# A softmax with relative bias: chunks of 6 rows in 4 buffers instead of 4 in 6, an evenly shared first load, and a drain of GpSimd's queue ahead of the end

## Chip, cores, metric

One core of a Trainium2 chip, all other cores idle. The metric is the device time of one execution in microseconds (us). "Span" is the time from the first to the last instruction in the profile; the measured time is some 1.6 to 2.0 us longer.

## The reference

```python
B, H, S = (2, 8, 2112)          # logits [B, H, S, S] float32, rel_bias [H, 33]
rel = clip(pos[:, None] - pos[None, :], -16, 16) + 16
x = logits + rel_bias[:, rel][None]
out = softmax(x, axis=-1)       # float32
```

Input and output are 285.5 MB each, so every element is loaded once and stored once: 571 MB in all.

## The kernel before

16 matrices of 2112 rows lie on 128 partitions, 264 rows to a partition. A chunk is `R` rows of every partition, in one of `BUFS` buffers. GpSimd's queue issues the loads, SyncE's the stores; VectorE adds the bias and scales, ScalarE takes exponentials with row sums. Within a chunk the work goes in parts of two rows, so that VectorE adds one part while ScalarE works on another. The maximum is not subtracted.

```python
    R = 4
    PARTS = [(0, 2), (2, R)]
    BUFS = 6
    N = T // R                       # T = 264 rows per partition
    ...
    def vec(eng, u, start, loads):   # VectorE
        eng.wait_ge(loaded[u], loads)
        for r0, r1 in PARTS:
            add(eng, u, r0, r1, start)
        for r0, r1 in PARTS:
            take(eng, summed, 1)
            ... reciprocal of the row sums ...
            for i in range(r0, r1):
                e = eng.tensor_scalar_mul(...)
        e.then_inc(scaled, 1)
    ...
    def sync_part(eng):
        row_load(eng, 0, R // 2, first)        # rows 0, 2 of the first chunk
        row_load(eng, 1, R // 2 - 1, first)    # row 1
        eng.wait_ge(loaded[BUFS - 2], 16)
        passes(eng, 0, lambda u, start, loads: store(eng, u, start))
        for n in range(BUFS):
            take(eng, stored[n], 16)

    def gpsimd_part(eng):
        row_load(eng, R - 1, 1, loaded[0])     # row 3
        ... two iotas ...
        for n in range(1, BUFS):
            if n == BUFS - 1:
                take(eng, made, 1)             # the last buffer is scratch until the bias strip is made
            load(eng, n, n * R)
        passes(eng, BUFS, lambda u, start, loads: reload(eng, u, start))
```

`take` waits for a semaphore and takes the count away again; `reload` waits until a buffer is stored and loads it anew. ScalarE's queue loads the small bias table first, VectorE makes the bias strip `F` out of it, and only then can the first add start.

Of the kernel before, what the change touches and what calls it, by code (L numbers as in the profile page):

```python
# [14 lines left out]
def kernel(  # L15
# [20 lines left out]
    P = 128  # L36
    B, H, S, S2 = logits.shape
# [4 lines left out]
    T = S // Q  # L42
    assert Q * B * H == P and T * Q == S and T % W == 0
    M = T // W
    R = 4
    PARTS = [(0, 2), (2, R)]
    BUFS = 6
    N = T // R
    assert N * R == T and N % BUFS == 0 and R % 2 == 0
    FW = S + T - 1  # L50
    NB = (FW - 2 * MR) // W
    assert NB * W + 2 * MR == FW
    RS = R * S

# [3 lines left out]
    one = const.tile([P, 1], FP32, tag="one", name="one")  # L58
    L = [const.tile([P, RS], FP32, tag=f"L{u}", name=f"L{u}") for u in range(BUFS)]
    tot = [const.tile([P, R], FP32, tag=f"tot{u}", name=f"tot{u}") for u in range(BUFS)]  # L60


    qi, mm, qm, eq, lt, gt, rest = (
        L[BUFS - 1][:, NB * m : NB * (m + 1)] for m in range(7)
    )
# [8 lines left out]
    section = ctx.enter_context(tc.tile_critical(name="rows"))  # L74
    loaded = [nc.alloc_semaphore(f"loaded{u}") for u in range(BUFS)]
    stored = [nc.alloc_semaphore(f"stored{u}") for u in range(BUFS)]
    table = nc.alloc_semaphore("table")
    blocks_ready = nc.alloc_semaphore("blocks_ready")
    strip = nc.alloc_semaphore("strip")
    first = nc.alloc_semaphore("first")  # L80
# [6 lines left out]
    def take(eng, sem, v):  # L87
        eng.wait_ge(sem, v).then_inc(sem, -v)  # L88

    def load(eng, u, start):  # L90
        eng.dma_start(out=L[u][:], in_=rows(logits, start)).then_inc(loaded[u], 16)  # L91

    def store(eng, u, start):
        take(eng, scaled, 1)
        eng.dma_start(out=rows(out, start), in_=L[u][:]).then_inc(stored[u], 16)

    def reload(eng, u, start):
        take(eng, stored[u], 16)
        load(eng, u, start)

    def add(eng, u, r0, r1, start):
        x = L[u]
        x3 = bass.AP(
            tensor=x.tensor,
            offset=x.offset + (r1 - 1) * S,
            ap=[[list(x.ap[0])[0], P], [-S, r1 - r0], [1, S]],
        )

        F3 = bass.AP(
            tensor=F.tensor,  # L110
            offset=(F.offset + T - r1) - start,
            ap=[[list(F.ap[0])[0], P], [1, r1 - r0], [1, S]],
        )
        eng.tensor_tensor(out=x3, in0=x3, in1=F3, op=ALU.add).then_inc(added, 1)  # L114

    def exps(eng, u):
        for r0, r1 in PARTS:
            take(eng, added, 1)
            for i in range(r0, r1):
                x = L[u][:, i * S : (i + 1) * S]  # L120
                e = eng.activation(out=x, in_=x, func=EXP, accum_out=tot[u][:, i : i + 1])  # L121
            e.then_inc(summed, 1)

    def vec(eng, u, start, loads):
# [5 lines that stand above are left out]
            t = tot[u][:, r0:r1]  # L130
            eng.reciprocal(out=t, in_=t).then_inc(inverted, 1)  # L131
            take(eng, inverted, 1)
            for i in range(r0, r1):
                x = L[u][:, i * S : (i + 1) * S]
                e = eng.tensor_scalar_mul(out=x, in0=x, scalar1=tot[u][:, i : i + 1])  # L135
        e.then_inc(scaled, 1)

    def passes(eng, n0, body):

        with eng.Fori(0, ((N - n0) // BUFS - 1) * 8 + 1, 8) as i:  # L140
            for n in range(n0, n0 + BUFS):
                body(n % BUFS, i * (BUFS * R // 8) + n * R, i * 2 + 16 * (n // BUFS + 1))

# [3 lines left out]
    def strip_of(eng):  # L147

        assert M * Q & (M * Q - 1) == 0
        low = rbP[:, W - 1 : W]  # L150
        high = rbP[:, 0:1]
        pitch = list(F.ap[0])[0]
        blocks = bass.AP(tensor=F.tensor, offset=F.offset + MR, ap=[[pitch, P], [W, NB], [1, W]])
        rev = bass.AP(
            tensor=rbP.tensor,
            offset=rbP.offset + W - 1,
            ap=[[list(rbP.ap[0])[0], P], [0, NB], [-1, W]],
        )

        def wide(t):  # L160
            return bass.AP(
                tensor=t.tensor, offset=t.offset, ap=[[list(t.ap[0])[0], P], [1, NB], [0, W]]
            )

        def step(ins):
            ins.then_inc(strip, 1)
            take(eng, strip, 1)

        take(eng, blocks_ready, 2)
        step(eng.tensor_single_scalar(out=qi, in_=qi, scalar=M * Q - 1, op=ALU.bitwise_and))  # L170
        step(eng.tensor_tensor(out=qm, in0=qi, in1=mm, op=ALU.subtract))  # L171
        for m, op in ((eq, ALU.is_equal), (lt, ALU.is_gt), (gt, ALU.is_lt)):
            step(eng.tensor_scalar(out=m, in0=qm, scalar1=0.0, scalar2=None, op0=op))  # L173
        take(eng, table, 16 * B)
        step(eng.tensor_scalar(out=rest, in0=lt, scalar1=low, scalar2=None, op0=ALU.mult))  # L175
        step(eng.tensor_copy(out=F[:, 0:MR], in_=low.to_broadcast([P, MR])))  # L176
        step(
            eng.scalar_tensor_tensor(  # L178
                out=rest, in0=gt, scalar=high, in1=rest, op0=ALU.mult, op1=ALU.add
            )  # L180
        )
        step(eng.tensor_copy(out=F[:, FW - MR : FW], in_=high.to_broadcast([P, MR])))  # L182
        step(eng.tensor_tensor(out=blocks, in0=wide(eq), in1=rev, op=ALU.mult))  # L183
        step(eng.tensor_tensor(out=blocks, in0=blocks, in1=wide(rest), op=ALU.add))  # L184
        eng.sem_inc(made, 1)

    def table_load(eng, bs):
        for b in bs:
            eng.dma_start(
                out=rbP[b * H * Q : (b + 1) * H * Q],  # L190
                in_=bass.AP(
                    tensor=rel_bias.tensor,
                    offset=rel_bias.offset,
                    ap=[[W, H], [0, Q], [1, W]],
                ),
            ).then_inc(table, 16)

    def row_load(eng, r0, m, sem):

        x = L[0]  # L200
        eng.dma_start(  # L201
            out=bass.AP(
                tensor=x.tensor,
                offset=x.offset + r0 * S,
                ap=[[list(x.ap[0])[0], P], [2 * S, m], [1, S]],
            ),
            in_=bass.AP(
                tensor=logits.tensor,
                offset=logits.offset + r0 * S,
                ap=[[T * S, P], [2 * S, m], [1, S]],  # L210
            ),
        ).then_inc(sem, 16)

    def sync_part(eng):

        row_load(eng, 0, R // 2, first)
        row_load(eng, 1, R // 2 - 1, first)
        eng.wait_ge(loaded[BUFS - 2], 16)
        passes(eng, 0, lambda u, start, loads: store(eng, u, start))
        for n in range(BUFS):  # L220
            take(eng, stored[n], 16)

    def gpsimd_part(eng):
        row_load(eng, R - 1, 1, loaded[0])
        eng.iota(qi, pattern=[[0, NB]], base=0, channel_multiplier=M).then_inc(  # L225
            blocks_ready, 1
        )
        eng.iota(mm, pattern=[[1, NB]], base=1 - M, channel_multiplier=0).then_inc(  # L228
            blocks_ready, 1
        )  # L230
        for n in range(1, BUFS):
            if n == BUFS - 1:
                take(eng, made, 1)
            load(eng, n, n * R)
        passes(eng, BUFS, lambda u, start, loads: reload(eng, u, start))

    def scalar_part(eng):
        table_load(eng, range(B))


        eng.activation(  # L241
            out=one, in_=nc.const_aps.tensor(0.0, [P, 1], FP32), func=EXP
        )
        passes(eng, 0, lambda u, start, loads: exps(eng, u))

    def vector_part(eng):
        strip_of(eng)
        take(eng, first, 32)
        passes(eng, 0, lambda u, start, loads: vec(eng, u, start, loads))

    sync_part(nc.sync)
    gpsimd_part(nc.gpsimd)
    scalar_part(nc.scalar)
    vector_part(nc.vector)


# [28 lines left out]
```

## Time and profile before

| | before |
|---|---|
| time, median of the first 3 runs | 1335.5 us (1335.49 to 1335.8) |
| span of the profiled run | 1333.3 us |
| VectorE / ScalarE busy | 72% / 40% |
| DMA, 200 to 1200 us | 433 GB/s, busy share 1.00 |
| last store landed / span ends | 1326.9 / 1333.3 us |

The page's DMA issues (queue and shape, KB each, median us from issue to landing):

```profile
out_dram<-L SPq DMA_DIRECT2D x66, 4224.0 KB, 71.0
L<-in_logits_dram POOLq DMA_DIRECT2D x65, 4224.0 KB, 31.8
```

A store takes 71 us from issue to landing. Shared with the loads its own transfer takes 20 us (10 alone), so some 2.5 stores are queued ahead of it. The windows view of the last stretch (us; busy time of VectorE, ScalarE, GpSimd; clock; DMA share; GB/s) shows what that queue is good for:

```profile
1290.00:1300.00 10.00, 7.76 (x7) 6.09 (x8) 0.00 (x0) 1.00 1.00 433
1300.00:1310.00 10.00, 0.00 (x0) 0.00 (x0) 0.00 (x0) 1.00 1.00 433
```

While VectorE finishes the last chunk (1290 to 1300) and for 20 us after it, DMA goes on at full rate out of the queue.

### The profile page before, as it was taken

The numbers are of one execution on the slowest core, as the hardware profiler recorded it, in microseconds if no ns is written. First come the engines' busy times: TensorE is split into PE (matmuls) and PEld (weight loads), VectorE is DVE, ScalarE is ACT, GpSimd is POOL, SyncE is SP. The second block draws the span as 40 slices with busy tenths as digits, with TensorE's granted clock in tenths as the row PEclk, the third lists the DMA queues.
The fourth block names the chain that finished last, engine by engine and source line by source line (L and its number), as shares of the span: only waits on it lengthen the run. The fifth ranks groups of instructions, "written<-read, shape, count | busy, mean of one in ns | idle before, by whom it ended". The sixth has DMA issues, their size and how long they took to land. A line of the windows view has us; busy time of VectorE, ScalarE, GpSimd; clock; DMA share; GB/s. (4 is left out here: it accounts for less than half of the span.)

```text
span 1333.3 us, 2515 instructions
## 1 busy us (share of the span) xinstructions
DVE 954.7 (72%) x539; ACT 529.8 (40%) x530; POOL 37.0 (3%) x72
## 2 busy tenths in 40 slices
DVE  2888888777677677677677677677677677677670
ACT  0444455444244244244244244344344343343340
POOL 1000000000000000000000000000000000000000
DMA  9999999999999999999999999999999999999996
GB/s 396 430 432 425 437 436 425 437 436 436 426 436 438 424 437 436 435 427 436 438 423 438 437 434 427 436 438 424 437 437 433 428 437 437 424 438 436 434 427 286
DMA packets 19571, 570.99 MB, mean 428 GB/s; under 512 B 2289, under 2 KB 2289, under 8 KB 2289
## 3 DMA queue, kind: packets, MB, share of 16 engines
q1 hardware_dynamic: 9920, 288.72, 50.2%
q0 software_dynamic: 9504, 282.24, 49.1%
q10 hardware_dynamic: 144, 0.02, 0.0%
q14 instruction: 3, 0.02, 0.0%
HBM read 285.49 MB, written 285.47 MB: 428 GB/s over the span
## 5 line engine op out<-in xcount | busy, mean ns | idle before, releaser
L121 ACT ACTIVATE L<-L 128x2112 f32<-128x2112 f32 x264 | 516.0, 1955 | 763.8 <-ACTq L88 763.8
L114 DVE TENSOR_TENSOR L<-L,F 128x4224 f32<-128x4224 f32 x132 | 595.7, 4554 | 201.0 <-DMA L<-in_logits_dram 200.2
L135 DVE TENSOR_SCALAR L<-L,tot 128x2112 f32<-128x2112 f32 x264 | 337.0, 1318 | 21.4 <-DVEq L88 6.1
L131 DVE RECIPROCAL tot<-tot 128x2 f32<-128x2 f32 x132 | 21.3, 162 | 98.3 <-DVEq L88 98.3
L91 POOL DMA_DIRECT2D L<-in_logits_dram x65 | 35.9, 552 | 1213.3 <-POOLq L88 1213.3
L121 ACT ACTIVATION_READ_ACCUMULATOR L<-L 128x1 f32 x264 | 49.2, 186 | 0.0
L175 DVE TENSOR_SCALAR L<-L,rbP 128x71 f32<-128x71 f32 x1 | 0.3, 258 | 19.9 <-DVEq L88 19.9
L183 DVE TENSOR_TENSOR F<-L,rbP 128x2343 f32<-128x2343 f32 x1 | 2.6, 2599 | 0.1
L184 DVE TENSOR_TENSOR F<-F,L 128x2343 f32<-128x2343 f32 x1 | 2.6, 2599 | 0.1
L241 ACT ACT_TABLE_LOAD x1 | 1.3, 1283 | 2.9 <-issue 2.9
L170 DVE TENSOR_SCALAR L<-L 128x71 int32<-128x71 int32 x1 | 0.2, 198 | 2.9 <-DVEq L88 2.9
L173 DVE TENSOR_SCALAR L<-L 128x71 f32<-128x71 f32 x3 | 0.7, 239 | 0.4
L201 POOL DMA_DIRECT2D L<-in_logits_dram x1 | 0.7, 664 | 1.1 <-PEq L280 1.1
L178 DVE SCALAR_TENSOR_TENSOR L<-L,rbP 128x71 f32<-128x71 f32 x1 | 0.3, 294 | 0.2 <-DVEq L88 0.2
L171 DVE TENSOR_TENSOR L<-L 128x71 f32<-128x71 int32 x1 | 0.2, 235 | 0.1
L182 DVE COPY F<-rbP 128x16 f32<-128x16 f32 x1 | 0.2, 175 | 0.1
L176 DVE COPY F<-rbP 128x16 f32<-128x16 f32 x1 | 0.2, 174 | 0.1
L225 POOL IOTA L<- 128x71 int32 x1 | 0.2, 208 | 0.1
L228 POOL IOTA L<- 128x71 int32 x1 | 0.2, 208 | 0.0
L241 ACT ACTIVATE one<-const-float32-0.0 128x1 f32<-128x1 f32 x1 | 0.2, 203 | 0.0
L269 POOL MEMSET const-float32-0.0<- 128x1 f32 x1 | 0.1, 99 | 0.4 <-issue 0.4
L269 POOL MEMSET const-bfloat16-1.0<- 128x1 bf16 x1 | 0.1, 102 | 0.0
(2 smaller groups left out, 0.2 us busy)
## 6 DMA issues: line engine op xcount, KB each, us to landing
out_dram<-L SPq DMA_DIRECT2D x66, 4224.0 KB, 71.0
L<-in_logits_dram POOLq DMA_DIRECT2D x65, 4224.0 KB, 31.8
L<-in_logits_dram SPq DMA_DIRECT2D x1, 2112.0 KB, 10.2
L<-in_logits_dram SPq DMA_DIRECT2D x1, 1056.0 KB, 22.6
L<-in_logits_dram POOLq DMA_DIRECT2D x1, 1056.0 KB, 10.1
rbP<-in_rel_bias_dram ACTq DMA_DIRECT2D x2, 8.2 KB
```

Source lines behind the costliest of these rows:

```text
L91: eng.dma_start(out=L[u][:], in_=rows(logits, start)).then_inc(loaded[u], 16)
L114: eng.tensor_tensor(out=x3, in0=x3, in1=F3, op=ALU.add).then_inc(added, 1)
L121: e = eng.activation(out=x, in_=x, func=EXP, accum_out=tot[u][:, i : i + 1])
L131: eng.reciprocal(out=t, in_=t).then_inc(inverted, 1)
L135: e = eng.tensor_scalar_mul(out=x, in0=x, scalar1=tot[u][:, i : i + 1])
L173: step(eng.tensor_scalar(out=m, in0=qm, scalar1=0.0, scalar2=None, op0=op))
L175: step(eng.tensor_scalar(out=rest, in0=lt, scalar1=low, scalar2=None, op0=ALU.mult))
L178: eng.scalar_tensor_tensor(out=rest, in0=gt, scalar=high, in1=rest, op0=ALU.mult, op1=ALU.add)
L183: step(eng.tensor_tensor(out=blocks, in0=wide(eq), in1=rev, op=ALU.mult))
L184: step(eng.tensor_tensor(out=blocks, in0=blocks, in1=wide(rest), op=ALU.add))
L201: eng.dma_start(out=bass.AP(tensor=x.tensor, offset=x.offset + r0 * S, ap=[[list(x.ap[0])[0], P], [2 * S, m], [1, S]],), in_=bass.AP(tenso ...
L241: eng.activation(out=one, in_=nc.const_aps.tensor(0.0, [P, 1], FP32), func=EXP)
```

## The change

The intent: fewer and larger transfers with the same SBUF (24 rows of buffer either way), a first chunk that both queues bring in equal halves, and GpSimd's queue drained as soon as its last load is issued.

```diff
-    R = 4
-    PARTS = [(0, 2), (2, R)]
-    BUFS = 6
+    R = 6
+    PARTS = [(0, 2), (2, 4), (4, R)]
+    BUFS = 4
@@ row_load: m rows, two apart -> R // 2 rows, two apart
@@ sync_part
-        row_load(eng, 0, R // 2, first)
-        row_load(eng, 1, R // 2 - 1, first)
+        row_load(eng, 0, first)
@@ gpsimd_part
-        row_load(eng, R - 1, 1, loaded[0])
+        row_load(eng, 1, loaded[0])
         ...
         passes(eng, BUFS, lambda u, start, loads: reload(eng, u, start))
+        eng.drain()
@@ vector_part
-        take(eng, first, 32)
+        take(eng, first, 16)
```

More of the change, by code (lines that the diff above doesn't have):

```diff
@@ L196, in table_load, with row_load @@
             ).then_inc(table, 16)
-    def row_load(eng, r0, m, sem):
+    def row_load(eng, r0, sem):
         x = L[0]
@@ L204, in row_load @@
                 offset=x.offset + r0 * S,
-                ap=[[list(x.ap[0])[0], P], [2 * S, m], [1, S]],
+                ap=[[list(x.ap[0])[0], P], [2 * S, R // 2], [1, S]],
             ),
@@ L209, in row_load @@
                 offset=logits.offset + r0 * S,
-                ap=[[T * S, P], [2 * S, m], [1, S]],
+                ap=[[T * S, P], [2 * S, R // 2], [1, S]],
             ),
```

## The prediction

> **What bounds the kernel now.** I read the page first, for which engine is full:
>
> ```profile
> span 1333.3 us, 2515 instructions
> DVE 954.7 (72%) x539; ACT 529.8 (40%) x530; POOL 37.0 (3%) x72
> ...
> DMA  9999999999999999999999999999999999999996
> ```
>
> VectorE is at 72%, ScalarE at 40%, and the DMA engines are busy in every slice but the last. The windows view puts figures on a middle stretch and on the end:
>
> ```profile
> 600.00:620.00 20.00, 14.36 (x8) 8.00 (x8) 0.53 (x1) 1.00 1.00 433
> ...
> 1313.00:1318.00 5.00, 0.00 (x0) 0.00 (x0) 0.00 (x0) 1.00 1.00 433
> 1318.00:1323.00 5.00, 0.00 (x0) 0.00 (x0) 0.00 (x0) 1.00 0.64 277
> 1323.00:1328.00 5.00, 0.00 (x0) 0.00 (x0) 0.00 (x0) 1.00 0.03 14
> 1328.00:1333.00 5.00, 0.00 (x0) 0.00 (x0) 0.00 (x0) 1.00 0.00 0
> ```
>
> The last columns are the DMA share and GB/s. The share is 1.00 at 433 GB/s with loads and stores mixed (600) and with stores alone (1313). 571 MB at 433 GB/s is 1,318.7 us, nearly the span. The rest is a start of about 2.2 us (the first packet in the trace's records starts at 2.2) and an end in which nothing moves: DMA falls off at about 1321.5, yet the span lasts to 1333.3. Twelve microseconds at the end want an explanation. Line 74 (the close of the critical section), asked for by itself, gives half of it:
>
> ```profile
> L74 ACTq DRAIN  x1: 13/13/13, 1327.0 to 1327.0; - x1
> L74 POOLq DRAIN  x1: 5446/5446/5446, 1327.0 to 1327.0; - x1
> L74 DVEq DRAIN  x1: 17/17/17, 1327.0 to 1327.0; - x1
> ```
>
> (min/median/max in ns, then first and last start.) All engines drain at 1327.0, and only GpSimd's takes 5.446 us. The DMA queue's waits agree:
>
> ```profile
> SPq L74 <- POOLq L74: 5.3, 1, 5.3
> ```
>
> So the end reads: 15 of 16 DMA engines finish the last store by 1323.2 and the sixteenth at 1326.9 (the increments of that store's semaphore), then 5.4 us of GpSimd drain, then 0.8 us of closing barriers. The measured 1335.5 is 2.2 us above the span; I take that as constant.
>
> VectorE is no bound: it waits for loads, short and often, in the waits view:
>
> ```profile
> DVE L L114 <- DMA L<-in_logits_dram: 200.2, 52, 3.9
> ```
>
> The kernel is therefore bound by the transfers themselves. A saving counts only at the head, in the tail, or per packet.
>
> **What the Trainium skill says.** (1) "DMA: Bandwidth & Descriptors", section "Where 436 GB/s comes from", gives a ceiling of 435.2 GB/s for 16 ports, and "Why small descriptors are slow (HBM only)" a fixed overhead of about 3 cycles per packet. The trace agrees in kind. By its packet records a packet of 8,448 B takes 319 ns and one of 33,792 B takes 1,251 ns (medians). The difference, 932 ns for 25,344 B, is 27.2 GB/s for one engine, 435 GB/s for 16, and leaves 8.4 ns fixed per packet: more than three cycles, but small. So size barely matters, and it is already known what a bigger packet can give. (2) Same page, section "Queues, rings and completion order": each DMA engine takes turns between queues, a packet at a time. The head agrees: the tiny table waits behind large packets and lands at 24.4 us. (3) "Perfetto Trace Analysis", section "Sequencer-only Instruction (DRAIN, etc)": the reported time of a DRAIN starts when its semaphore wait is satisfied. So 5.446 us is execution, not waiting. I found no page that says why GpSimd's drain is long after DMA issues. (4) "DMA: Bandwidth & Descriptors", section "Latency and other measured facts", says that engines 7 and 15 are usually slower. The trace has one engine that lags (3.7 us on the last store); it does not show which.
>
> **The change part by part.**
>
> *Drain ahead of the end.* GpSimd has nothing left after its last load (issued at 1251.26). A drain placed there runs beside some 70 us of transfers. The one at line 74 remains, but has nothing new to do; GpSimd's further drains in the closing barriers take 34 to 78 ns. Gain: 5.4 us, all on the path that sets the end.
>
> *Bigger chunks: packets.* A chunk has 8 partitions per DMA engine (128/16) and each partition's run is one packet. Before: 33,792 B; after: 6 x 8,448 = 50,688 B, by the two durations above 319 + 5 x 310.7 = 1,872 ns, my estimate. Per engine before: first chunk 4 x 8 = 32 packets of 319 ns = 10.2 us; then 65 loads and 66 stores x 8 = 1,048 x 1.251 = 1,311.0; sum 1,321.3. After: 48 x 0.319 = 15.3; (43 + 44) x 8 = 696 x 1.872 = 1,303.2; sum 1,318.5. Gain 2.8 us. The 4-byte semaphore packets (9 ns) fall from 134 to about 89 per engine: 0.4 us. Together 3.2 us, on the path, because DMA is the bound.
>
> *Bigger chunks: VectorE and ScalarE.* The same 132 adds of 4.55 us, 264 multiplies of 1.32 us and 264 exponentials of 1.96 us. Where chunks are not starved, VectorE has fewer chunk ends at which it waits for ScalarE (1.5 us each at present). All of this lies beside transfers: nothing.
>
> *First chunk shared evenly.* Now three rows on each queue, all in small packets. The table's 18 small packets per participating engine wait one round each; a round is 0.32 + 0.32 us while both queues hold small packets, instead of 0.32 + 1.25 us later on. I expect the table at about 16 us instead of 24.4, the first add at about 24 instead of 32.2, and the first store ready near 24 + 22 = 46. SyncE then waits for chunk 2 (18 rows, 19.5 MB at 433 GB/s: 45 us, so about 48). The fourth load, issued at 24, keeps DMA busy meanwhile: it was busy before and is busy after. Gain on the path: nothing. The extra small packets are in the sum already.
>
> *Four buffers: does DMA ever run out?* A period is 24 rows, 120 us, as before. A chunk is 22.8 us in the engines (worked out below), so about 97 us of each buffer's period are in DMA, and one chunk takes 30 us in each direction when both are mixed: about three chunks are always queued. No.
>
> *Tail.* Here it is tight. Before, the last chunk was:
>
> ```profile
> 1283.40 9.03 DVE L114 TENSOR_TENSOR L<-L,F 128x4224 f32<-128x4224 f32 x2 [3.88 <-DMA L<-in_logits_dram]
> ...
> 1297.01 2.55 DVE L135 TENSOR_SCALAR L<-L,tot 128x2112 f32<-128x2112 f32 x2
> 1299.80 0.33 SPq L95 DMA_DIRECT2D out_dram<-L  x1
> ```
>
> Landing (1283.1) to store was 16.7 us; the stores then queued lasted far longer. After: three adds end at 13.6; the third exponential pair runs 13.7 to 17.7; multiplies of parts one and two fill 13.9 to 19.4; the third reciprocal and multiplies end at 22.3; with the two hand-overs (0.28, 0.24) 22.8 us, plus about 1.1 to the first packet: 24. Work left when the last load lands: a store completes about 10 to 12 us ahead of each load landing (11 to 12.5 in the trace), so the next store has had half of that in DMA time, leaving 15 - 5.5, plus one whole store of 15: about 24.5 us. Just covered. I allow +0.3 us, with 2 us possible.
>
> Sum: 1335.5 - 5.4 - 3.2 + 0.3 = 1327.2.
>
> **Rivals.** *The early drain buys nothing*: the long drain may be a cost of waking GpSimd after a long idle, or of anything that follows its DMAs, so that the last drain is long again. The only long drain in the trace is both first after DMA issues and after 75 us of idleness, so the trace cannot tell. The short ones that follow directly speak for "nothing new to do". I give this rival one in five; it makes the time 1332.6.
>
> *The tail opens*: with only four buffers, the load's latency may come out longer, and fewer stores are left to hide 24 us of compute. DMA would stand idle for 1 to 3 us late. One in four: 1328 to 1330.
>
> *Packets of 50,688 B are slower, or are cut*: nothing in the trace has this size. Cut in two they would give 25,344 B packets of 0.94 us, 1.33 times as many as before instead of two thirds: 1,392 x 0.940 = 1,309 us instead of 1,303, some 6 us worse than predicted. If the row pitch in HBM met some conflict it could be 2% or more; but 33,792 B packets show none. One in twelve.
>
> *The faster start pays on the path*: for it, 8 us of earlier compute; against it, the DMA share of 1.03 and 1.05 in the windows from 10 to 30 us, when compute does not run at all. Worth 0.
>
> *The lagging engine*: it sets the end, 3.7 us behind the fifteenth. Its lag grows in the mixed stage only; if per packet, it shrinks by a third (-1 us), if per turn between large packets it grows by half (+2).
>
> **Range and chances.** The main case is 1327.2, with about 1 us either side for lag and packets; the drain rival and the open tail stretch the upper side to 1332.5. I give 1327.3, 1324.8 to 1332.6. Two per cent is 26.7 us: faster would need 1308.8, and 571 MB at 435.2 GB/s alone take 1,312, so it is out of reach; slower needs a fault of the large packets. Faster 0.01, within 0.97, slower 0.02.
>
> **What would show it.** A short GpSimd drain at line 74 (under 0.1 us) and a long one at the new line, 70 us or more ahead of the end: the drain step right. 33,792 B records replaced by 50,688 B ones of 1.87 us, and some 435 GB/s in the middle: the packet step. First add near 24 us with an unchanged DMA share in the first 50 us: the head is worth nothing. DMA share 1.00 from the last load's landing until the fall, and the last store issued before the previous one lands: no hole in the tail. I am wrong if the time is above 1333 (drain and packets both void), or below 1324 (something saved that I do not see).

## The result, and the profile after

| | before | after |
|---|---|---|
| time, median (range) | 1335.49 us (1333.25 to 1335.8, 4 runs) | 1328.0 us (1325.86 to 1330.2, 4 runs) |
| ratio, 95% interval | | 0.9948 (0.9925 to 0.997) |
| span of the profiled run | 1333.3 | 1328.6 |
| time of the profiled run | 1335.23 | 1330.2 |

A ratio is the mean time of one kernel's fast runs over that of the other's of the same rounds, so it is not quite the ratio of the medians quoted beside it. Two later calls (chips 7 and 11) ran the same changed kernel again: medians 1329.89 and 1330.02, beside 1335.51 and 1335.76 for the kernel before, so the gain there is 5.6 to 5.7 us and not 7.5. The 15 runs of the changed kernel spread from 1325.9 to 1335.4, those of the kernel before from 1332.9 to 1336.6. The profile below is of the slowest of the first four runs, which is near the later medians; no run near 1326 was traced.

The page of the changed kernel:

```profile
span 1328.6 us, 2321 instructions
...
DVE 946.9 (71%) x539; ACT 529.8 (40%) x530; POOL 44.0 (3%) x50
...
DMA  9999999999999999999999999999999999999997
...
out_dram<-L SPq DMA_DIRECT2D x44, 6336.0 KB, 53.7
L<-in_logits_dram POOLq DMA_DIRECT2D x43, 6336.0 KB, 42.7
```

Still DMA-bound, with the same work on VectorE. A store now takes 53.7 us, of which its own transfer is 30 when shared (15 alone): only 0.8 of a store is queued ahead of it, 12 us of work instead of 25. Line 74, where the critical section closes, and line 238, the added drain (ns, then start in us):

```profile
L74 POOLq DRAIN  x1: 47/47/47, 1327.5 to 1327.5; - x1
```

```profile
L238 POOLq DRAIN  x1: 45987/45987/45987, 1244.6 to 1244.6; - x1
```

The long drain has moved: it runs from 1244.6 to 1290.6, beside the transfers, and the one at the end takes 0.047 us. The same middle stretch (200 to 1200 us) asked of the DMA view, first of the kernel before, then of the changed one:

```profile
DMA packets 14421, 433.05 MB, mean 433 GB/s; under 512 B 1606, under 2 KB 1606, under 8 KB 1606
```

```profile
DMA packets 9628, 433.69 MB, mean 434 GB/s; under 512 B 1072, under 2 KB 1072, under 8 KB 1072
```

A third fewer packets move 0.15% more bytes in the same 1000 us. Over 1,320 us that would be 2.0 us, not the 3.2 predicted; but the window is a coarse measure, as c_r4_rest (below), with the packets of the kernel before, moved 433.39 MB in it, half of the difference. The head came earlier as foretold: by the timeline the first add starts at 25.05 us instead of 32.23. And the tail, in the windows view:

```profile
1290.00:1300.00 10.00, 10.00 (x3) 5.85 (x5) 0.00 (x0) 1.00 1.01 436
1300.00:1310.00 10.00, 9.55 (x10) 6.15 (x8) 0.00 (x0) 1.00 0.46 198
1310.00:1315.00 5.00, 0.81 (x1) 0.00 (x0) 0.00 (x0) 1.00 0.76 324
```

From 1300 to 1310, where the kernel before ran at 433 GB/s with its compute already done, the changed one moves less than half of that while VectorE is still at the last chunk. This is a hole. The timeline gives its cause: the last chunk's first add waits for its load until 1289.0, and its last multiplies end at 1310.8.

```profile
1289.00 13.50 DVE L114 TENSOR_TENSOR L<-L,F 128x4224 f32<-128x4224 f32 x3 [8.17 <-DMA L<-in_logits_dram]
...
1308.26 2.55 DVE L135 TENSOR_SCALAR L<-L,tot 128x2112 f32<-128x2112 f32 x2
```

The increments of the store semaphores tell how the 16 DMA engines stand (each store raises its semaphore in 16 steps, which I read as one for each engine whose share has landed):

| | first | 15th | 16th |
|---|---|---|---|
| before, last store but one | 1311.75 | 1313.25 | 1316.94 |
| before, last store | 1321.72 | 1323.21 | 1326.90 |
| after, last store but one | 1305.04 | 1307.31 | 1311.29 |
| after, last store | 1327.22 | 1327.37 | 1327.40 |

After the change, all engines wait for the last store, which is issued at 1311.04; its first packets start at 1311.9. The fastest engine has been idle for about 7 us by then, the slowest for 1.1 (both from the packet records). So the hole costs the end only what the slowest engine sees of it.

**Where the 4.7 us of span went.** A store of 6 rows takes 15.0 us alone. Without hole, the fastest engine would have ended at 1305.0 + 15.0 = 1320.0 instead of 1321.7: 1.7 us less transfer time, which every engine has. The slowest would have ended at 1311.3 + 15.0 = 1326.3 instead of 1326.9: its lag behind the fastest has grown from 5.2 to 6.2 us, which takes back 1.1. The hole takes the other 1.1: the store lands at 1327.4. So transfers and tail together end 0.5 us **later** than before. All that is gained in the span comes after them: from landing to the end of the span 6.4 us before, 1.2 after, which is the drain's 5.4 less 0.2 of closing steps that it had covered. 0.3 us more is gained outside the span (time minus span 1.95 before, 1.65 after). The drain is not the reason, as a_drain_only and c_r4_rest (4 rows, with the drain) have 2.05; what is, no run shows.

### The profile page after: what moved, and what is told of

The parts are those of the page before. It is cut to its first block, busy times and chain, and to the rows that moved or that the text cites. A ratio compares the mean times of both kernels' runs of the same rounds, so it can differ in the third digit from the quotient of the medians.

```text
span 1328.6 us, 2321 instructions
## 1 busy us (share of the span) xinstructions
DVE 946.9 (71%) x539; ACT 529.8 (40%) x530; POOL 44.0 (3%) x50
## 5 line engine op out<-in xcount | busy, mean ns | idle before, releaser
L91 POOL DMA_DIRECT2D L<-in_logits_dram x43 | 42.6, 991 | 1200.0 <-POOLq L88 1200.0
L204 POOL DMA_DIRECT2D L<-in_logits_dram x1 | 0.9, 880 | 1.1 <-PEq L283 1.1
## 6 DMA issues: line engine op xcount, KB each, us to landing
out_dram<-L SPq DMA_DIRECT2D x44, 6336.0 KB, 53.7
L<-in_logits_dram POOLq DMA_DIRECT2D x43, 6336.0 KB, 42.7
```

Source lines behind the costliest of these rows:

```text
L91: eng.dma_start(out=L[u][:], in_=rows(logits, start)).then_inc(loaded[u], 16)
L204: eng.dma_start(out=bass.AP(tensor=x.tensor, offset=x.offset + r0 * S, ap=[[list(x.ap[0])[0], P], [2 * S, R // 2], [1, S]],), in_=bass.AP( ...
```

## The experiments

All twelve runs were timed in 5 rounds beside the kernel before, in three calls (a_, b_, c_, each on another chip), and every result was correct. Theory at the start: the drain is worth its 5.4 us, the packets about 2, and the hole in the tail costs about 1 and makes the times scatter. Rivals: the drain's gain comes from elsewhere (fewer transfers, or the head); the packets are worth the predicted 3.2; the scatter has nothing to do with the hole.

### a_change: the changed kernel again

> The whole change again, on this chip, to see how much the times spread from run to run on one chip. If the two levels seen so far (1326 and 1330) belong to the chip, these runs agree within 1 us; if they belong to the run, both levels show here. The trace should again have a DMA hole of about 1 us on the slowest DMA engine and 5 to 7 us on the others before the last store.

Measured: 1329.89 us (1328.77 to 1332.89, 5 runs; before 1335.51; ratio 0.996, 0.9948 to 0.9973). A scatter of 4 us is there on one chip, so that much belongs to the run; but the level of 1326 did not come back in these runs or in the six of c_change, so of the two levels this settles nothing. In this trace the slowest engine had no hole (it finished the last store but one at 1312.1, after the last store's issue at 1309.95); the fastest idled from 1304.9 on. Lag first to last 6.85 us. So in these two traces the time is about the same with and without a hole on the slowest engine (spans 1328.6 and 1328.2): where there was no hole, the lag was larger.

### a_drain_only

```diff
 (kernel before)
         passes(eng, BUFS, lambda u, start, loads: reload(eng, u, start))
+        eng.drain()
```

> The kernel before with nothing but the drain added. Theory (drain leaves the end): 5.4 us faster than before, about 1330.1, with a GpSimd drain under 0.1 us at the close of the critical section. Rival (the long drain belongs to any drain that follows a long idle): same time as before, and a drain of about 5.4 us still there.

Measured: 1330.54 us (1330.4 to 1331.14; ratio 0.9963, 0.995 to 0.9976), 5.0 us less than before. Its lines 74 and 236 (the drain):

```profile
L74 POOLq DRAIN  x1: 47/47/47, 1327.5 to 1327.5; - x1
```

```profile
L236 POOLq DRAIN  x1: 34518/34518/34518, 1251.8 to 1251.8; - x1
```

The theory holds, the rival of a wake-up after idleness falls: GpSimd has been idle for 41 us ahead of its last drain here, and it is short. One added line gives nearly the whole difference between the two kernels.

### a_no_drain

```diff
 (changed kernel)
-        eng.drain()
```

> The change without the drain. Theory: 5.4 us slower than the change, about 2 us faster than before. If the length of the drain goes with the number of GpSimd's transfers since the start (45 instead of 66), the last drain takes about 3.7 us; if it is a constant, 5.4 us.

Measured: 1334.51 us (1330.48 to 1341.25, 6 runs; ratio 1.0001, 0.9981 to 1.0022): 4.6 us slower than the change by the medians, and no different from the kernel before. The 2 us below the kernel before that I had expected did not show; with runs that lie 11 us apart they are not ruled out either. The drain at the end:

```profile
L74 POOLq DRAIN  x1: 3652/3652/3652, 1327.0 to 1327.0; - x1
```

At these two counts the length goes with the number of transfers that GpSimd issued: 3,652 ns for 44, 5,446 ns for 66, both 83 ns each (the count is 1 row load and 43 loads here, 1 and 65 before). So larger chunks alone would have shortened the end by 1.8 us, and the early drain takes the remaining 3.65. Where the drain is placed behind the last load, it ends 1.85 us (44 transfers, changed kernel) or 2.74 us (66, a_drain_only) after that load has landed, so 42 ns for each: it waits for the transfers that are under way. A third count shows that this is no general rule: in c_r2_rest (below), with 132 transfers, the drain ended 1.28 us after the last load had landed, and not 5.5.

### a_even_only

```diff
 (kernel before)
-        row_load(eng, 0, R // 2, first)
-        row_load(eng, 1, R // 2 - 1, first)
+        row_load(eng, 0, R // 2, first)
@@
-        row_load(eng, R - 1, 1, loaded[0])
+        row_load(eng, 1, R // 2, loaded[0])
@@
-        take(eng, first, 32)
+        take(eng, first, 16)
```

> The kernel before with nothing but the even split of the first chunk (2 rows and 2 rows). Theory (DMA is the bound from the first microseconds): table and first add come several us earlier, the time stays within 1 us of before. Rival (an earlier start of VectorE reaches the end): 5 us or more faster.

Measured: 1336.19 us (1335.57 to 1337.04; ratio 1.0005, 0.9992 to 1.0017). The timeline shows that the head did what it should, 9 us ahead of the kernel before:

```profile
23.21 9.03 DVE L114 TENSOR_TENSOR L<-L,F 128x4224 f32<-128x4224 f32 x2 [0.81 <-DVEq L88]
```

And nothing of it reached the end (0.7 us slower by the medians, within the interval). The even split is worth nothing, as predicted.

### b_split_store

The last pass is written out behind the loop (SyncE and VectorE), and the last chunk is stored by parts:

```diff
 (changed kernel, last chunk)
-        store(eng, u, start)
+        for r0, r1 in PARTS:
+            take(eng, scaled, 1)         # given after each part's multiplies
+            eng.dma_start(out=rows(out, (N - 1) * R + r0, (r1 - r0) * S),
+                          in_=L[BUFS - 1][:, r0 * S : r1 * S]).then_inc(stored[BUFS - 1], 16)
```

> The change, with the last chunk's store cut into three, each sent as soon as its two rows are scaled, so the last 15 us of stores start some 6 us sooner after the last load lands. Theory (a hole ahead of the last store, 0 to 1.4 us on the slowest DMA engine and 5 to 7 us on the others, is what makes the change's runs scatter): no hole in the trace on any engine longer than 1 us, 0 to 1.5 us faster than the change (1328.5 to 1330), and runs that agree within 1.5 us instead of 4. Rival (the scatter comes from elsewhere): the same scatter of 4 us, no gain.

Measured: 1329.36 us (1328.81 to 1333.41; ratio 0.9959, 0.9946 to 0.9972). The hole is smaller, 313 GB/s in place of 198; on the fastest engine it is 2.9 us instead of 7, still more than the 1 us that I had allowed:

```profile
1300.00:1310.00 10.00, 9.55 (x9) 7.75 (x8) 0.00 (x0) 1.00 0.73 313
1310.00:1315.00 5.00, 2.40 (x2) 0.00 (x0) 0.00 (x0) 1.00 1.00 426
```

The scatter stayed at 4.6 us, so my theory of the scatter falls. The profiled run was the slowest of the five (1333.41), and in it two engines came late: the last store but one had its first increment at 1305.3, its 15th at 1314.5 and its 16th at 1315.7. The lag of one or two engines differs from trace to trace, and in this run it set the time: 15.0 us of stores after 1315.7 end at 1330.6, where the last increment came. That it moves the time of the untraced runs too is likely, not shown. By the medians the closed hole gains 0.5 to 0.7 us over the change of the other two calls, which is within the scatter.

### b_act_loads and b_act_split

All loads move from GpSimd's queue to ScalarE's; the reload for chunk n + 2 is issued after the exponentials of chunk n. The second kernel has the split store as well.

```diff
 (changed kernel, scalar_part, abridged)
-        passes(eng, 0, lambda u, start, loads: exps(eng, u))
+        for n in range(2):
+            exps(eng, n)
+        passes(eng, 2, both)             # both: exps(u); reload((u + 2) % BUFS, start + 2 * R)
+        for n in range(N - 2, N):
+            exps(eng, n % BUFS)
```

> The change with all loads issued from ScalarE's queue (hardware descriptors) instead of GpSimd's; GpSimd issues no transfer and is not drained. Theory (one DMA engine lags 4 to 6 us behind because of GpSimd's descriptors): all 16 increments of the last stores and loads come within about 1 us, and the time falls by the lag, 3 to 5 us below the change, to 1325 to 1327. Rival (the lag belongs to the DMA engine or to where the data lies): the last increment still comes 3 to 5 us after the fifteenth, and the time is that of the change, about 1330.

> Both: loads from ScalarE's queue and the last store in three pieces. Without the lag the hole ahead of the last store would stand open on all engines (some 1 to 3 us), so the split should give that on top of b_act_loads: 1323 to 1325. If the lag stays, about as b_split_store.

Measured: b_act_loads 1332.84 us (1329.22 to 1335.95, 6 runs; ratio 0.9979), b_act_split 1329.72 us (1329.25 to 1331.48; ratio 0.9961). The lag did not go; in this the rival was right, while the time of b_act_loads was nearer 1333 than its 1330. In the profiled run of b_act_loads the last store but one had its 15th increment at 1306.3 and its 16th at 1314.8, a lag of 8.5 us with no GpSimd transfer in the kernel; in b_act_split 4.2 us. In this trace the lag is also what makes the hole:

```profile
1300.00:1310.00 10.00, 9.85 (x5) 9.07 (x11) 0.00 (x0) 1.00 0.42 182
1310.00:1315.00 5.00, 4.70 (x7) 2.03 (x3) 0.00 (x0) 1.00 0.05 20
```

The last load has landed only when the slowest engine has brought its share (1294.1 here, ten us after the fastest), so compute starts late, and all engines but one run dry. So here the lag is paid a second time, as little is queued behind the last load.

### b_row_packets

Every store is cut into two strided halves (even rows, odd rows), so its packets are single rows of 8,448 B.

> The change with every store in two strided halves, so that stores move in packets of 8,448 B and not 50,688 B: 1,760 more packets per DMA engine, nothing else changed. With 8.4 ns per packet (the records' durations, as predicted) 14.8 us slower than the change; with 5.2 ns (durations less the 3 ns by which neighbouring records overlap) 9.2 us; with nothing per packet, the same time.

Measured: 1346.32 us (1345.34 to 1349.34; ratio 1.0086, 1.0073 to 1.0099), 16.4 us slower than a_change of another call, more than either figure. The middle stretch:

```profile
DMA packets 31079, 427.61 MB, mean 428 GB/s; under 512 B 1583, under 2 KB 1583, under 8 KB 1583
```

The packet records split the 16.4. Load packets (50,688 B, unchanged) take longer than 1,872 ns by 158 us in sum over 16 engines, 9.9 us per engine; in the changed kernel 1.1. The longer ones, by 0.1 to 0.7 us for the most part, are nearly all (454 of 472) the last packet of a load on its engine. A load of large packets now lands in a median of 23.7 us beside stores of small ones (42.7 in the changed kernel), and then the load queue is empty until the next load. Why the last packets take longer is not shown. If they lengthen the run by their mean, they account for 8.8 us. The remaining 7.6 over 1,760 packets (44 more semaphore packets per engine are in it) are 4.3 ns per packet. This fits how the records lie: within one DMA engine the next packet's record starts most often 4 ns before the last one ends, so of the 8.4 ns that the durations give, 4.4 are left. The experiment is less clean than it was meant to be, as it changed the sharing of the queues too; so the 4.3 ns is an estimate from the records, not a measurement by itself.

### c_change, c_r4_rest

The change once more, and the change with `R`, `PARTS` and `BUFS` as before.

> The change once more, as the partner of the other runs of this call: about 1330, with a scatter of some 4 us.

> The change with the chunk size alone put back to 4 rows in 6 buffers (drain and even split stay). Theory (the fewer packets save 1.8 us on every DMA engine, but the slowest engine's larger lag takes most of it back): 1330.5, within 1 us of the change, with a scatter under 1.5 us and a last lag of 3.5 to 4.5 us. Rival (the packet step holds in full): 3.2 us slower than the change, 1333.

Measured: c_change 1330.02 us (1328.8 to 1335.43, 6 runs; ratio 0.9965, 0.9951 to 0.9978); c_r4_rest 1330.97 us (1330.08 to 1331.74, 5 runs; ratio 0.9964, 0.9952 to 0.9977). The chunk size as such is worth nothing that these runs can tell: 1 us by the medians, nothing by the means. The rival of 3.2 us falls. In the traces both sides of the sum are seen: the fastest engine would have ended its last store (without the hole) at 1305.0 + 15.0 = 1320.0, and ended it at 1322.2 with 4 rows, so 2.2 us are saved; but the last store landed at 1326.95 and 1327.84, only 0.9 us apart. The rest is hole: the slowest engines were free at 1310.4 and the last store's first packets started at 1311.4 to 1311.6.

### c_r2_rest

```diff
 (changed kernel)
-    R = 6
-    PARTS = [(0, 2), (2, 4), (4, R)]
-    BUFS = 4
+    R = 2
+    PARTS = [(0, R)]
+    BUFS = 12
```

> The same with 2 rows in 12 buffers: packets of 16,896 B, some 1,040 more per DMA engine than with 4 rows, and 132 more semaphore packets. With 4.4 ns per packet (durations less an overlap of 4 ns) and 5 ns per semaphore: 5.2 us slower than the 4-row kernel of this call, 1335.7. With 8.4 and 9 ns, as predicted: 9.9 us slower, 1340.

Measured: 1562.19 us (1561.78 to 1562.92; ratio 1.1695). A miss of mine, and no answer on packets: with one part to a chunk, VectorE has nothing to do while ScalarE works, and waits at every reciprocal. The waits view and a window say so:

```profile
DVE tot L131 <- DVEq L88: 565.1, 132, 4.7
```

```profile
600.00:620.00 20.00, 12.88 (x7) 6.57 (x7) 0.65 (x2) 1.00 0.93 365
```

Add 4.55, wait 4.3, multiplies 2.55 and hand-overs make some 11.7 us for 2 rows, where DMA needs 10. The engines have become the bound, and 132 chunks of 11.7 are 1,544 of the 1,561 us span. What this shows instead: without parts VectorE comes onto the path; the kernels with two or three parts to a chunk stay bound by DMA.

### c_serial_tail

The last chunk alone is worked in one part of 6 rows (adds, then exponentials, then multiplies); all else as in the change.

> The change with the last chunk alone worked in one part (all adds, then all exponentials, then all multiplies), which lengthens its compute by about 11.5 us. Theory (with four buffers the stores queued behind the last load only just cover its compute on the slowest DMA engine): 9.5 to 11.5 us slower than the change. Rival (the backlog still hides it, as 13 us of slack did in the kernel before): under 2 us slower.

Measured: 1339.32 us (1336.41 to 1343.73, 6 runs; ratio 1.0031, 1.0017 to 1.0045), 9.3 us slower than c_change, just under the range that I gave and far from the rival's 2. Load landed 1284.9, store issued 1318.75: 33.9 us of compute. In its windows the hole has spread to all engines:

```profile
1300.00:1310.00 10.00, 0.00 (x0) 10.00 (x12) 0.00 (x0) 1.00 0.45 193
1310.00:1315.00 5.00, 4.14 (x5) 0.18 (x2) 0.00 (x0) 1.00 0.00 2
```

So in the changed kernel more compute in the last chunk lands on the path that sets the end: of some 11.5 us more, 9.3 were paid. The trace of the kernel before has room for that: its last store was issued at 1299.8, 12 us before even the fastest engine had landed its share of the store ahead of it (1311.75). This room is what the change gave up.

## Why the prediction was right, and where not

The time was inside the range, 0.7 us above the figure (and 2.6 to 2.7 in the later calls); the class, too, was right. That the first call came so close is partly luck. Its profiled run, 1330.2, lies next to what the rival of the opening tail (one in four) gave, 1328 to 1330, and in it hole and lag took back all that the packets gave. What the untraced runs at 1325.9 and 1326.5 did better is not known. Its steps:

- **DMA is the bound, so the engines' work and the head are worth nothing.** Right. a_even_only brought the first add 9 us forward and the time not at all.
- **Drain: 5.4 us.** Right in mechanism and size: 5.0 us with the drain alone. The rival of one in five (a wake-up after idleness) was refuted. What I could not know from one trace: the length is 83 ns per GpSimd transfer, at 44 and at 66. My reading that a DRAIN's reported time is execution and not waiting went too far: the early drain's 45,987 ns last until 1.85 us after the last load has landed, so waiting for transfers is in it.
- **Packets: 3.2 us.** Right in mechanism, mis-sized. It measured 1.7 us (fastest engine, before against after) to 2.2 us (c_r4_rest against c_change). The term took the whole duration of a record as time of the engine, although records overlap by 4 ns; 336 fewer packets (1,080 less 744, the first chunk counted) x 4.4 ns and 45 semaphore packets of about 5 ns are 1.7 us, an estimate from the records. The numbers were in the trace before: from 200 to 1200 us its two queues' packets fill 50.2% and 50.1% of the engines' time, more than 100%.
- **Tail: +0.3 us, up to 2.** The mechanism (compute of the last chunk against the stores behind it) was right, shown by c_serial_tail. In the profiled run the hole was 1.1 us on the slowest engine, and in that of a_change there was none. My balance of 24.5 against 24 us came out as about 22 against 23.
- **Lag of the slowest engine: unchanged but for 1 us either way.** The weakest step. It grew by about 1 us in the profiled run (5.2 to 6.2 us, first to last engine; behind the fifteenth, as the prediction counts it, 3.7 to 4.0); the other two profiles of the changed kernel show 6.9 and 5.7, its variants with 6 rows 4.1 to 10.4, the four profiled 4-row kernels 5.2 to 5.7. In the profiled run it took back, together with the hole, all that the packets gave.
- **My test for the tail was badly chosen.** "The last store issued before the previous one lands" came true (1311.04 against 1311.29), though 15 of 16 engines stood idle. A landing shows the slowest engine; the DMA share shows the others.
- **Time minus span: 2.2 us, constant.** It was 1.95 before and 1.65 after. The 2.2 had set the median of other runs against the profiled span.

What stays open is why the lag is larger and less steady with 6 rows. The traces show a difference: after 200 us, not one packet of the four profiled 4-row kernels with 33,792 B packets takes over 0.1 us longer than the median, while in each of the eight 6-row kernels whose packets are 50,688 B 19 to 69 do. A lag needs no such packets: in the kernel before, the last engine falls behind evenly, by 0.42 us in 100 us (first to last increment of a store, 2.8 us at 727 us and 4.8 at 1206). But in the profiled run of the changed kernel the slow engine loses 0.2 us in 100 us up to 879 and after 1178, and 2.8 us between 879 and 1148, and all 19 of that run's longer packets lie between 852 and 1148. (Until 969 this engine is the fifteenth to land, after that the sixteenth; that it is one engine is read from the curve, as the trace does not name it.) So in this trace the longer packets come together with the added lag; which causes which, and what lengthens them, no run here tells. Nor is it shown that it is always the same DMA engine that lags; b_act_loads shows only that GpSimd's transfers are not needed for it.

No version tried beats the changed kernel clearly. Set against the change of its own call, the kernel before with the drain, alone or with the even split, is as fast by the means and steadier: 1330.1 to 1331.7 in the 10 runs of a_drain_only and c_r4_rest, against 1325.9 to 1335.4 in the 15 of the change.

## What to carry to other kernels

If GpSimd issues transfers, look at the close of the kernel for its DRAIN: one placed behind its last transfer hid a cost of 3.6 us with 44 transfers and 5.4 with 66. In a kernel bound by transfers, a chunk size is judged by its tail: what is queued behind the last load must outlast the compute of the last chunk, and it must do so on the slowest DMA engine, which lands the load late. Per-packet costs read off durations are too high where records overlap; compare instead when the fastest engine has finished the same work.

## What the Trainium skill lacked or had wrong

- No page has the length of GpSimd's DRAIN after it has issued transfers: 5,446 ns for 66 and 3,652 ns for 44, 83 ns each (other counts were not tried at the end); 47 ns if one was placed behind the last transfer.
- "VectorE: DVE Perf Modes", section "The DRAIN you can't avoid", tells two sorts apart: the flush after a VectorE instruction, and the runtime's own DRAINs, about 12 ns on all 5 engines. It has no word on the DRAINs at the close of a kernel's critical section: here SyncE's took 7, ScalarE's 13 and VectorE's 17 ns, but GpSimd's 47 to 5,446.
- "DMA: Bandwidth & Descriptors", section "Latency and other measured facts", says that engines 7 and 15 are usually slower, and as a best guess puts it down to GpSimd's descriptors. In b_act_loads, where GpSimd issues no transfer, the last engine came 8.5 us after the fifteenth, so an engine can lag without them. Whether it is one of those two, the runs do not show.
- The same page, "Where 436 GB/s comes from", says that between HBM and SBUF the HBM side binds at about 358 GB/s, though it notes a measurement of 425 beside it. With one core at work, that limit did not bind: loads and stores together ran at 433 to 434 GB/s from 200 to 1200 us.
